# Two-layer encoder trunk: low halves of the last score tile padded to 128 rows, the boundary's norms issued one or two steps earlier, other PSUM banks for the third output tile

## The chip, the core and the metric

One core of one Trainium2 chip runs the whole kernel. The metric is the device time of one execution in microseconds, from the profiler's clock; lower is better. Three runs of the kernel before took 1560.03, 1561.87 and 1566.96 us, so the median is 1561.87 us.

## What is computed

Two layers over 528 tokens (16 meta tokens and 512 of input) of width 1024, in float32. Each layer norms the tokens, projects them to ten pieces, runs a gated short convolution and a chunkwise retention side by side, merges them by sigmoid gates, projects back with `w_o`, norms that and adds it to the residual. Cut to what matters here:

```python
for l in range(DEPTH):
    xn = _rmsnorm(h, pre_norm_g[l])
    proj = xn @ w_in[l] + b_in[l]
    ...
    y_b = _retention_branch(r_q, r_k, r_v, r_z, ret_gn_g[l], w_ret_out[l])
    y = jax.nn.sigmoid(g_a) * y_a + jax.nn.sigmoid(g_b) * y_b
    y = y @ w_o[l]
    h = h + _rmsnorm(y, post_norm_g[l])
return h[:, N_META:]
```

In the retention branch the queries and keys of a head give scores, the scores are weighted by a decay table, and the weighted scores multiply the values. Four heads per layer, 512 value columns per head.

## The kernel before

**Precision.** Every float32 operand of a large product is split into a high half (a rounded copy, written by ScalarE) and a low half (the rest, written by VectorE), by `split` (L140 to L143). A product is then three passes on TensorE: high by high, high by low, low by high. In the names of the profile `whi` and `wlo` are the halves of a weight, `Xh` and `Xl` those of the layer's input, `Shi` and `Slo` those of a head's scores.

**Work of a layer.** TensorE goes through a fixed list of jobs: `Group` (two input projections by a seven-product block scheme, L279), `RetOut` and `ConvOut` (L244), and at the layer's end the product with `w_o` (L678). Small steps that belong to a job, such as norms, scores (`scores`, L425), value transposes (`vtrans`, L450) and the product of scores and values (`attend`, L484), are put into a queue with a delay: `later(d, fn)` lets `fn` be issued d ticks later, and a tick falls every twelve matmuls or so (`mul`, `mm_tile`, `Std.run`, `wo_half`, `opening` call `tick`). The framework then orders the instructions of each engine by priority and by when it thinks their operands are there, and gives out the buffers. Each engine runs its own list in order.

**Scores by values.** A head's keys lie in five tiles, `JT`; the last, j = 4, has 64 real keys. For it the value tile holds the keys twice: in rows 0 to 63 and again in rows 64 to 127, with the high values above the low ones in `V[4][1]`. So two passes are enough: `V[4][1]` by `Shi` over 128 rows, and `V[4][0]` by `Slo` over 64 rows, which is what these lines of `attend` say:

```python
passes = ((0, 0), (0, 1), (1, 0)) if j < len(JT) - 1 else ((1, 0), (0, 1))
...
if j == len(JT) - 1 and x == 0:
    kn = CHUNK
```

`attend` runs four times per head (once for 128 value columns), so 4 x 4 x 2 = 32 times in all, and the 64-row pass is its last matmul each time.

**The boundary between the layers.** `wo_half` multiplies by `w_o` for the first half of the tokens, then for the second (half 0, half 1). `norms` queues for each half a chain with these steps: `tok("y")` sums squares over the channels with small matmuls (`rstd_token`, L370), VectorE scales the sum (L374) and GpSimd takes the power -0.5 (L375); `spread` puts the factor on all partitions with six small matmuls (L384) and ScalarE copies it out (L387); `resid` scales, adds to the residual and squares (L782, L787, L669, L671); then the same statistics and spread for the next layer's norm (`tok("h")`, `spread`), and `scaled` writes the next layer's input halves (L791, then L142 and L143). `opening` starts the first products of layer 1 on half 0, then on half 1, and needs the halves that `scaled` wrote.

**The tail.** The last layer's product with `w_o` (L1167) takes tokens in four tiles of 128. Tiles 0 and 1 fill both buffers of the PSUM pool `pp` (two banks each) in an interleaved loop; tiles 2 and 3 then run one after the other, each half of the columns in a bank of `pp`. `begin` (L1183, L1188) reads a bank out on ScalarE and VectorE. The single banks `pa` and `pc` are used by the input projections and idle in the tail.

Of the kernel before, what the change touches and what calls it, by code (L numbers as in the profile page):

```python
# [11 lines left out]
F32 = mybir.dt.float32  # L12
# [3 lines left out]
ALU = mybir.AluOpType  # L16
# [11 lines left out]
CHUNK = 64  # L28
HALF = T // 2
# [13 lines left out]
JT = [(0, 80, 0), (80, 128, 80), (208, 128, 208), (336, 128, 336), (464, 128, 464)]  # L43
SOFF = [0, 528, 976, 1296, 1488]
# [12 lines left out]
def trunk(ctx: ExitStack, tc: tile.TileContext, xT, w_in, binT, w_co, w_ro, w_o, gpre, gpost,  # L57
          gpost_row, convw, convb, gng, cosT, sinT, decay, out):
    nc = tc.nc
# [13 lines left out]
    def nm(s):  # L73
        cnt[0] += 1
        return f"{s}{cnt[0]}"
# [7 lines left out]
    def pslot():  # L83
        return ps.tile([P, 2, 512], F32, tag="pp", name=nm("pp"))

    def bank(tag):
        return ps1.tile([P, 512], F32, tag=tag, name=nm(tag), bufs=2 if tag == "pb" else 1)
# [39 lines left out]
    def later(delay, fn):  # L127
        now[1] += 1
        heappush(queue, (now[0] + delay, now[1], fn))
# [11 lines left out]
    def split(dst_hi, dst_lo, src):  # L141
        nc.scalar.copy(dst_hi, src)  # L142
        nc.vector.tensor_tensor(dst_lo, src, dst_hi.bitcast(F32), op=ALU.subtract)  # L143
# [140 lines left out]
    class Group:  # L284
# [19 lines left out]
        def halves(self, j):  # L304
            if j != 1:
                r = self.raw[j]
                nc.vector.tensor_tensor(r[:, 512:], r[:, 512:], r[:, 0:512], op=ALU.add)  # L307
            self.w[j] = wtile("whi"), wtile("wlo")
            split(*self.w[j], self.raw[j])
# [68 lines left out]
    def spread(dst, y, t0, sc, nch):  # L378

        pp = pslot()  # L380
        per = min(nch, 264 // sc)
        nb = nch // per
        for c in range(nch):
            nc.tensor.matmul(pp[:, c // per, (c % per) * sc:(c % per + 1) * sc], y[:, c:c + 1].to_broadcast([sc, P]),  # L384
                             ident[0:sc, 0:sc], start=True, stop=True)
        with tc.high_priority():
            nc.scalar.copy(dst[:, t0:t0 + nch * sc].rearrange("p (a b) -> p a b", a=nb), pp[:, 0:nb, 0:per * sc])  # L387
# [27 lines left out]
    def scores(l, q, k, k8, Shi, Slo, js):  # L415

        pp = pslot()
        todo = []
        for n, j in enumerate(js):
            k0, kn, q0 = JT[j]  # L420
            cols = QCOLS[l] if j == 0 else Cols(q0, T - q0, 1)
            for dt in range(2):
                for a, (x, y) in enumerate(((0, 0), (0, 1), (1, 0))):
                    for i, sl in cols.pieces():
                        nc.tensor.matmul(  # L425
                            pp[0:kn, n + i, 0:cols.n], k[dt][x][:, k0:k0 + kn] if j < 4 else k8[:, dt * 2 + x, :], q[dt][y][:, sl],
                            start=(dt == 0 and a == 0), stop=(dt == 1 and a == 2),
                        )
            todo.append((n, j, cols))
        for n, j, cols in todo:  # L430
            k0, kn, q0 = JT[j]
            o = cols.t0 - q0
            s = fslot()
            sv = s[0:kn, 0:cols.w]
            with tc.high_priority():
                nc.vector.tensor_tensor(
                    sv.rearrange("p (a b) -> p a b", a=cols.np),
                    pp[0:kn, n:n + cols.np, 0:cols.n],
                    Dsb[0:kn, DOFF[j] + o:DOFF[j] + o + cols.w].rearrange("p (a b) -> p a b", a=cols.np),
                    op=ALU.mult)  # L440
            ss = slice(SOFF[j] + o, SOFF[j] + o + cols.w)
            later(1, lambda kn=kn, ss=ss, sv=sv: split(Shi[0:kn, ss], Slo[0:kn, ss], sv))

    def vtrans(vt, v8, V, js):

# [20 lines left out]
    def attend(l, h, Shi, Slo, V, v, t, sums):  # L466


        banks = [(0, 208), (208, 528)] if l < DEPTH - 1 else [(META, T)]
        pp = pslot()  # L470
        todo = []
        for j, (k0, kn, q0) in enumerate(JT):
            passes = ((0, 0), (0, 1), (1, 0)) if j < len(JT) - 1 else ((1, 0), (0, 1))
            for x, y in passes:
                for b, (s0, s1) in enumerate(banks):
                    lo_, hi_ = max(s0, q0), s1
                    if lo_ < hi_:
                        todo.append((j, x, y, b, lo_, hi_))
        for n, (j, x, y, b, lo_, hi_) in enumerate(todo):
            _, kn, q0 = JT[j]  # L480
            if j == len(JT) - 1 and x == 0:
                kn = CHUNK
            S = (Shi, Slo)[y]
            nc.tensor.matmul(  # L484
                pp[:, b, lo_ - banks[b][0]:hi_ - banks[b][0]],
                V[j][x][0:kn, v * P:(v + 1) * P],
                S[0:kn, SOFF[j] + lo_ - q0:SOFF[j] + hi_ - q0],
                start=not any(t[3] == b for t in todo[:n]),
                stop=not any(t[3] == b for t in todo[n + 1:]),
            )  # L490
        sq = sums if v == 0 else fslot()
        g = gn_sb[:, l, h * 4 + v:h * 4 + v + 1]
        with tc.high_priority():
            for b, (s0, s1) in enumerate(banks):
                nc.scalar.activation(sq[:, s0:s1], pp[:, b, 0:s1 - s0], AF.Square)
            for b, (s0, s1) in enumerate(banks):
                nc.vector.scalar_tensor_tensor(t[:, s0:s1], pp[:, b, 0:s1 - s0], g, t[:, s0:s1], op0=ALU.mult, op1=ALU.mult)
            if v:
                qs = slice(banks[0][0], T)
                nc.vector.tensor_tensor(sums[:, qs], sums[:, qs], sq[:, qs], op=ALU.add)  # L500
# [271 lines left out]
    def norms(l, half, hts, ysum, hsum, R2, R):  # L772

        sl = slice(half * HALF, (half + 1) * HALF)
        st = {}

        def tok(key, sums):
            st[key] = rstd_token(sums, half * HALF, 88, 3)

        def scale(k):  # L780
            y = YB[:, k:k + 4, sl]
            nc.vector.tensor_tensor(y, y, R2[:, sl].unsqueeze(1).to_broadcast([P, 4, HALF]), op=ALU.mult)  # L782

        def resid(k):
            if k % 4 == 0:
                scale(k)
            nc.vector.tensor_tensor(hts[k][:, sl], hts[k][:, sl], YB[:, k, sl], op=ALU.add)  # L787
            squares(k, hts[k][:, sl], sl, hsum)

        def scaled(k):  # L790
            nc.vector.scalar_tensor_tensor(YB[:, k, sl], hts[k][:, sl], gpre_sb[:, l + 1, k:k + 1], R[:, sl],  # L791
                                           op0=ALU.mult, op1=ALU.mult)
            split(*plain(half, k), YB[:, k, sl])

        later(2, lambda: tok("y", ysum))
        later(5, lambda: spread(R2, st["y"], half * HALF, 88, 3))
        for k in range(KD):
            later(5, lambda k=k: resid(k))
        later(13, lambda: tok("h", hsum))
        later(16, lambda: spread(R, st["h"], half * HALF, 88, 3))  # L800
        for k in range(KD):
            later(16, lambda k=k: scaled(k))

    def opening(tiles, half, ts):

# [20 lines left out]
    for l in range(DEPTH):  # L826
# [7 lines left out]
        hd = heads(0)  # L834
# [27 lines left out]
        def q_done(ts, hd, h, l, d=8):  # L862
            a, b, hd["q"] = rope(ts, QCOLS[l].t0)
            later(0, a)
            later(2, b)

            def tables():
                hd["S"] = [gr.tile([P, SW], F32R, tag="S", name=nm(x), bufs=2) for x in ("Shi", "Slo")]
                nc.sync.dma_start(Dsb, decay[h])
            later(3, tables)  # L870
            for n, js in enumerate(((0,), (1, 2), (3, 4))):
                later(d + 2 * n, lambda js=js: scores(l, hd["q"], hd["k"], hd["k8"], *hd["S"], js))
# [102 lines left out]
    pa = bank("pa")  # L975
    warm = bank("pc")
    for n in range(9):
        o, a, b = (warm, 0, P) if n < 6 else (pa, (n - 6) * P, min((n - 5) * P, HALF))
# [10 lines left out]
    for ks in (slice(0, 1), slice(1, 2), slice(2, 4), slice(4, 6), slice(6, 8)):  # L989
        nc.sync.dma_start(YB[:, ks, :], xT[ks].rearrange("k p t -> p k t"))  # L990
        j = ks.start // 4
# [4 lines left out]
    for k in range(KD):  # L996
        for half in range(2):
            prescale(0, k, half, YH[:, k, half, :])
        j, kk = k // 4, slice(k % 4 * P, (k % 4 + 1) * P)
# [15 lines left out]
    for n in range(3):  # L1015
        t = fslot()
# [6 lines left out]
    R = fslot()  # L1023
# [11 lines left out]
    hd = jobs[0][0]  # L1035
# [40 lines left out]
    for l in range(DEPTH):  # L1076
# [4 lines left out]
        if l:  # L1081
            hd = jb[0]
# [43 lines left out]
        if not last:  # L1126
# [6 lines left out]
            hsum = gr.tile([P, T + 2], F32, tag="u", name="hsum", bufs=2)[:, 0:T]  # L1133
            R2 = fslot()
            R = fslot()
# [15 lines left out]
        else:  # L1151
# [62 lines left out]
            for t in range(2, SEQ // P):  # L1214
                st = state()
                for half in range(2):
                    o = pslot()[:, 0, :]
                    for k in range(KD):
                        wo_k(o, t, k, half)
                    begin(st, o, half)  # L1220
                if t == 2:
                    finish(sts[0], 0)
                    finish(sts[1], 1)
                finish(st, t)
# [80 lines left out]
```

## Time and profile before

| | |
|---|---|
| runs | 1560.03, 1561.87, 1566.96 us, median 1561.87 us |
| profiled execution | 1560.22 us, its span 1558.4 us |
| TensorE matmul busy | 1537.1 us, 99% of the span |
| VectorE busy | 1166.1 us, 75% |
| ScalarE busy | 912.2 us, 59% |
| GpSimd busy | 18.8 us, 1% |
| DMA | 174.37 MB, 112 GB/s on average |

A matmul's duration in the profile overlaps that of the next one, so the distance between two starts, not the duration, is what a matmul costs. Weight loads have rows of their own (PEld) and normally run beside the matmul before.

### The profile page before, as it was taken

The page shows a single profiled execution, that of the slowest core. Times are in us where ns is not written, and L with a number is a line of the kernel's source. Part 1 is how long each engine was busy: PE and PEld are TensorE (multiplying, and loading weights), DVE is VectorE, ACT ScalarE, POOL GpSimd, SP SyncE. Part 2 cuts the span into 40 slices and gives each one's busy share as a digit, 9 for nine tenths or more (in the row PEclk, how much of TensorE's full clock was granted, in tenths as well). Part 3 has the DMA queues.
Part 4 walks back from the last instruction along what each step waited for, and adds up shares of the span by engine and source line. Part 5 has one row for each costly group of instructions (what it writes and reads, how often), then busy time and mean ns, then how long its engine had stood idle before and what let it go on. Part 6 is the DMA issues. An engine that isn't in the chain of part 4 may idle for free.

```text
span 1558.4 us, 29296 instructions
## 1 busy us (share of the span) xinstructions
PE 1537.1 (99%) x11762; PEld 1487.0 (95%) x11762; DVE 1166.1 (75%) x1702; ACT 912.2 (59%) x1763; POOL 18.8 (1%) x23
## 2 busy tenths in 40 slices
PE   9999999999999999999999999999999999999997
PEld 9999999999999999999999999999999999999986
DVE  6997776886878788857367987769778777996642
ACT  6685665565465467646345766655755655776521
POOL 0000000000000000000000000000000000000000
PEclk9999999999999999999999999999999999999999
DMA  8132332232232333435321223322322323334421
GB/s 270 57 128 75 116 109 96 102 110 91 97 106 89 116 122 125 140 129 181 107 104 62 102 95 109 116 98 99 122 95 89 109 97 120 136 131 141 145 88 54
DMA packets 86039, 174.37 MB, mean 112 GB/s; under 512 B 11280, under 2 KB 15888, under 8 KB 85904
## 3 DMA queue, kind: packets, MB, share of 16 engines
q1 hardware_dynamic: 85760, 172.50, 32.0%
q8 instruction: 92, 1.51, 0.4%
q14 instruction: 43, 0.35, 0.1%
q10 hardware_dynamic: 144, 0.01, 0.0%
HBM read 168.21 MB, written 4.26 MB: 111 GB/s over the span
## 4 chain that ended last, share of the span: by engine, by line
PE 91%; DVE 4%; ACT 2%; DMA 1%; issue 1%; SPq 0%; DVEq 0%; POOLq 0%; ACTq 0%
PE pb L279 29%; PE pp L244 18%; PE pc L279 15%; PE pa L279 7%; PE pp L678 7%; PE pp L484 4%; PE pb L678 3%; PE pp L1167 3%; PE pp L425 2%; DMA raw<-in_w_in 1%; PE pp L450 1%; DVE wlo L143 1%; PE pp L384 1%; PE pp L370 1%; ACT whi L142 1%
## 5 line engine op out<-in xcount | busy, mean ns | idle before, releaser
L143 DVE TENSOR_TENSOR wlo<-raw,whi 128x1024 fp32r<-128x1024 f32 (+2 forms) x358 | 394.0, 1109 | 136.9 <-ACT whi L142 135.3
L142 ACT CAST whi<-raw 128x1024 fp32r<-128x1024 f32 (+2 forms) x358 | 339.7, 959 | 251.1 <-PE pp L244 66.2
L279 PE MATMUL pb<-Xh,whi 128*128 128x264 f32 (+2 forms) x1008 | 289.9, 288 | 3.5 <-ACT pa L335 2.3
L279 PE MATMUL pb<-Xh,wlo 128*128 128x264 f32 (+2 forms) x1008 | 285.7, 283 | 0.0
L279 PE MATMUL pb<-Xl,whi 128*128 128x264 f32 (+2 forms) x1008 | 285.4, 283 | 0.0
L244 PE MATMUL pp<-r,whi 128*128 128x264 f32 (+1 forms) x1152 | 246.1, 321 | 0.0
L279 PE MATMUL pc<-Xh,whi 128*128 128x264 f32 (+2 forms) x672 | 193.8, 288 | 1.8 <-ACT f L325 1.5
L279 PEld LDWEIGHTS pb<-Xh,whi 128*128 128x128 f32 x1008 | 189.8, 188 | 5.7 <-ACT pa L335 3.1
L244 PEld LDWEIGHTS pp<-r,whi 128*128 128x128 f32 x1152 | 177.8, 188 | 15.9 <-ACT whi L142 0.3
L279 PE MATMUL pc<-Xl,whi 128*128 128x264 f32 (+2 forms) x672 | 190.7, 284 | 0.0
L279 PEld LDWEIGHTS pb<-Xl,whi 128*128 128x128 f32 x1008 | 189.8, 188 | 0.6
L279 PE MATMUL pc<-Xh,wlo 128*128 128x264 f32 (+2 forms) x672 | 190.3, 283 | 0.0
L279 PEld LDWEIGHTS pb<-Xh,wlo 128*128 128x128 f32 x1008 | 189.8, 188 | 0.0
L244 PE MATMUL pp<-r,wlo 128*128 128x264 f32 (+1 forms) x576 | 153.2, 321 | 0.0
L307 DVE TENSOR_TENSOR raw<-raw 128x512 f32<-128x512 f32 x168 | 115.3, 688 | 27.8 <-DMA raw<-in_w_in 27.0
L279 PEld LDWEIGHTS pc<-Xh,whi 128*128 128x128 f32 x672 | 126.6, 188 | 3.4 <-ACT f L325 2.8
L279 PEld LDWEIGHTS pc<-Xl,whi 128*128 128x128 f32 x672 | 126.6, 188 | 0.1
L279 PEld LDWEIGHTS pc<-Xh,wlo 128*128 128x128 f32 x672 | 126.5, 188 | 0.0
L244 PEld LDWEIGHTS pp<-r,wlo 128*128 128x128 f32 x576 | 95.5, 188 | 7.9
L314 DVE TENSOR_TENSOR raw<-raw,raw 128x512 f32<-128x512 f32 x84 | 58.0, 690 | 57.6 <-DMA raw<-in_w_in 57.4
L279 PE MATMUL pa<-Xh,whi 128*128 128x264 f32 (+2 forms) x336 | 96.8, 288 | 0.0
L279 PE MATMUL pb<-Xh,whd 128*128 128x264 f32 (+2 forms) x336 | 96.3, 287 | 0.3 <-ACT f L325 0.3
(219 smaller groups left out, 3324.0 us busy)
## 6 DMA issues: line engine op xcount, KB each, us to landing
raw<-in_w_in SPq DMA_DIRECT2D x426, 256.0 KB, 2.9
raw<-in_w_ro SPq DMA_DIRECT2D x32, 512.0 KB, 3.2
raw<-in_w_in SPq DMA_DIRECT2D x20, 512.0 KB, 5.0
raw<-in_w_co SPq DMA_DIRECT2D x16, 512.0 KB, 3.2
raw<-in_w_o SPq DMA_DIRECT2D x16, 512.0 KB, 3.8
Dsb<-in_decay SPq DMA_DIRECT2D x8, 520.0 KB, 4.6
h1d<-f SPq DMA_DIRECT2D x8, 264.0 KB, 4.2
f<-h1d SPq DMA_DIRECT2D x8, 264.0 KB, 5.1
```

The source lines that it names most:

```text
L142: nc.scalar.copy(dst_hi, src)
L143: nc.vector.tensor_tensor(dst_lo, src, dst_hi.bitcast(F32), op=ALU.subtract)
L244: nc.tensor.matmul(banks[i][:, 0:cols.n], wt(k)[:, msl], xs(k)[:, sl], start=(k == 0 and a == 0), stop=(k == nk - 1 and a == 2),)
L279: nc.tensor.matmul(o[:, 0:n], wt[:, k, :], xs[:, blk, k, HALF - n:], start=(first and k == 0 and a == 0), stop=(k == 3 and a == 2), skip_g ...
L307: nc.vector.tensor_tensor(r[:, 512:], r[:, 512:], r[:, 0:512], op=ALU.add)
L314: nc.vector.tensor_tensor(b[:, 0:512], a[:, 512:], c[:, 0:512], op=ALU.add)
L370: nc.tensor.matmul(pp[0:sc, 0, c:c + 1], sums[:, t0 + c * sc:t0 + (c + 1) * sc], ones_d[:, 0:1], start=True, stop=True)
L384: nc.tensor.matmul(pp[:, c // per, (c % per) * sc:(c % per + 1) * sc], y[:, c:c + 1].to_broadcast([sc, P]), ident[0:sc, 0:sc], start=True, ...
L425: nc.tensor.matmul(pp[0:kn, n + i, 0:cols.n], k[dt][x][:, k0:k0 + kn] if j < 4 else k8[:, dt * 2 + x, :], q[dt][y][:, sl], start=(dt == 0 ...
L484: nc.tensor.matmul(pp[:, b, lo_ - banks[b][0]:hi_ - banks[b][0]], V[j][x][0:kn, v * P:(v + 1) * P], S[0:kn, SOFF[j] + lo_ - q0:SOFF[j] + h ...
L678: nc.tensor.matmul(o, wt(k), xs[:, i0:], start=(k == 0 and a == 0), stop=(k == KD - 1 and a == 2))
L1167: nc.tensor.matmul(o, x[:, xs], wo[k][half][w], start=(k == 0 and a == 0), stop=(k == KD - 1 and a == 2))
```

## The change

1. In `scores`, the low half of the last key tile is written for 64 rows instead of 128, and a GpSimd memset in `tables` fills its rows 64 to 127 with zeros when a head's score tiles are opened. `attend` no longer cuts that pass to 64 rows, so all its matmuls for the last tile take 128 rows.
2. In `norms` the delays become smaller: spread and residual 5 to 4, the statistics of the next norm 13 to 12, their spread and the scaling 16 to 14. This holds for both halves.
3. In the tail, the two halves of tile 2 go to banks `pc` and `pa` instead of two buffers of `pp`.

```diff
-            later(1, lambda kn=kn, ss=ss, sv=sv: split(Shi[0:kn, ss], Slo[0:kn, ss], sv))
+            def halves(kn=kn, ss=ss, sv=sv, n=CHUNK if j == len(JT) - 1 else kn):
+                nc.scalar.copy(Shi[0:kn, ss], sv)
+                nc.vector.tensor_tensor(Slo[0:n, ss], sv[0:n], Shi[0:n, ss].bitcast(F32), op=ALU.subtract)
+            later(1, halves)
...
-            if j == len(JT) - 1 and x == 0:
-                kn = CHUNK
...
-        later(5, lambda: spread(R2, st["y"], half * HALF, 88, 3))
+        later(4, lambda: spread(R2, st["y"], half * HALF, 88, 3))
         for k in range(KD):
-            later(5, lambda k=k: resid(k))
-        later(13, lambda: tok("h", hsum))
-        later(16, lambda: spread(R, st["h"], half * HALF, 88, 3))
+            later(4, lambda k=k: resid(k))
+        later(12, lambda: tok("h", hsum))
+        later(14, lambda: spread(R, st["h"], half * HALF, 88, 3))
         for k in range(KD):
-            later(16, lambda k=k: scaled(k))
+            later(14, lambda k=k: scaled(k))
...
+                nc.gpsimd.memset(hd["S"][1][CHUNK:, SOFF[4]:].bitcast(F32), 0.0)
...
-                    o = pslot()[:, 0, :]
+                    o = bank(("pc", "pa")[half]) if t == 2 else pslot()[:, 0, :]
```

How the order of instructions moves. On TensorE, half 0: the spread of y stands 12 matmuls of L678 earlier than before, the statistics of h 13 and their spread 24. For half 1 the statistics of y stand 21 such matmuls later, their spread 12 earlier, the statistics of h 12 and their spread 24 earlier. Outside the boundary and the tail TensorE's order is the same. The first place is TensorE at the end of the product with `w_o` for half 1, where the statistics of h for half 0 are taken; `pp_9648` and `pp_9652` hold the output columns 4 and 5 before and after the change, `pp_9705` and `pp_9717` the columns 6 and 7, and `hsum` is the sum of squares. Before:

```order
L678 MATMUL pp_9705<-r_8935,Xh 128x264
L678 MATMUL pp_9705<-r_8937,Xh 128x264
L678 MATMUL pp_9705<-r_8935,Xl 128x264
L678 MATMUL pp_9705<-Xh,wos_8902 128x264
L370 MATMUL pp_9718<-ones_d,hsum 88x1 [waits DVE_49,Activation_49]
L678 MATMUL pp_9705<-Xl,wos_8902 128x264
L678 MATMUL pp_9705<-Xh,wos_8903 128x264
```

Now:

```order
L680 MATMUL pp_9652<-Xl,r_9193 128x264
L680 MATMUL pp_9652<-Xh,r_9194 128x264
L370 MATMUL pp_9701<-ones_d,hsum 88x1 [waits DVE_49,Activation_49]
L680 MATMUL pp_9717<-r_8938,Xh 128x264 [waits DVE_49]
L680 MATMUL pp_9717<-r_8940,Xh 128x264
```

The statistics moved ahead of columns 6 and 7, whose first matmul now waits for VectorE.

The second place is ScalarE from there to the first inputs of layer 1: L769 (now L771) and L669 (now L671) empty columns 6 and 7, L387 copies the spread factor of half 0, and the casts `Xh<-YB` write the high halves that `opening` reads. Before:

```order
L142 CAST Xh<-raw_9207 128x512 [waits PE_49]
L142 CAST Xh<-raw_9209 128x512 [waits PE_49]
L769 ACTIVATE YB<-pp_9705,gpost_sb 128x264 [waits PE_49]
L387 COPY f_9262<-pp_9762 128x264 [waits DVE_49,PE_49]
L669 ACTIVATE f_9792<-pp_9705 128x264 [waits DVE_49]
L769 ACTIVATE YB<-pp_9705,gpost_sb 128x264
L669 ACTIVATE f_9796<-pp_9705 128x264 [waits DVE_49]
L142 CAST Xh<-YB 128x264 [waits DVE_49] x8
```

Now:

```order
L387 COPY f_9266<-pp_9742 128x264 [waits DVE_49,PE_49]
L142 CAST Xh<-raw_9187 128x512 [waits PE_49]
L142 CAST Xh<-raw_9197 128x512 [waits PE_49]
L142 CAST Xh<-YB 128x264 [waits DVE_49] x4
L142 CAST Xh<-raw_9211 128x512 [waits PE_49]
L771 ACTIVATE YB<-pp_9717,gpost_sb 128x264 [waits PE_49]
L671 ACTIVATE f_9796<-pp_9717 128x264 [waits Activation_49]
L771 ACTIVATE YB<-pp_9717,gpost_sb 128x264
L671 ACTIVATE f_9800<-pp_9717 128x264
L142 CAST Xh<-YB 128x264 [waits DVE_49] x3
```

The copy and four of the eight casts now stand ahead of the emptying of columns 6 and 7.

The third place is TensorE at the start of token tile 2 in the tail; `pp_18019` and `pp_18027` are token tile 1. Before:

```order
L1167 MATMUL pp_18019<-r_17997,Xh 128x512
L1167 MATMUL pp_18019<-r_17996,Xl 128x512
L1167 MATMUL pp_18192<-Xh,r_17849 128x512 [waits DVE_49]
L1167 MATMUL pp_18192<-Xl,r_17849 128x512
L1167 MATMUL pp_18192<-Xh,r_17851 128x512
```

Now:

```order
L1170 MATMUL pp_18027<-r_18005,Xh 128x512
L1170 MATMUL pp_18027<-r_18004,Xl 128x512
L1170 MATMUL pc_18200<-Xh,r_17857 128x512
L1170 MATMUL pc_18200<-Xl,r_17857 128x512
L1170 MATMUL pc_18200<-Xh,r_17859 128x512
```

The order of the matmuls is the same; the wait for VectorE is gone.

On GpSimd the eight memsets stand ahead of a norm's power each, except the first.

## Rows read from the trace of the kernel before

**Rows 1.** The page: busy time by engine; the chain that ended last, by engine.
```profile
PE 1537.1 (99%) x11762; PEld 1487.0 (95%) x11762; DVE 1166.1 (75%) x1702; ACT 912.2 (59%) x1763; POOL 18.8 (1%) x23
...
PE 91%; DVE 4%; ACT 2%; DMA 1%; issue 1%; SPq 0%; DVEq 0%; POOLq 0%; ACTq 0%
```

**Rows 2.** Waits of TensorE for a norm's sums: total us, times, longest us.
```profile
PE pp L370 <- DVE f L500: 1.7, 2, 1.5
```

**Rows 3.** Groups by line and shape: the last key tile's two passes (busy us, mean ns).
```profile
L484 PE MATMUL pp<-Slo,r 64*128 64x64 f32 x32 | 9.4, 294 | 0.0
...
L484 PE MATMUL pp<-Shi,r 128*128 128x64 f32 x32 | 6.9, 216 | 0.0
```

**Rows 4.** Timeline, an attend's end: start us, us, what, matmuls and weight loads.
```profile
119.93 0.33 PE L484 MATMUL pp<-Shi,r 128*128 128x192 f32 x2
120.19 0.29 PE L484 MATMUL pp<-Slo,r 64*128 64x64 f32 x1
120.41 0.39 PE L279 MATMUL pa<-Xh,whi 128*128 128x264 f32 x1
120.64 0.28 PE L279 MATMUL pa<-Xl,whi 128*128 128x264 f32 x1
...
120.19 0.18 PEld L484 LDWEIGHTS pp<-Slo,r 64*128 64x128 f32 x1
```

**Rows 5.** Timeline, scores of the last key tile: weight loads, then the next two matmuls.
```profile
884.32 0.86 PEld L425 LDWEIGHTS pp<-r,r 128*128 128x128 f32 x7
...
885.13 0.37 PE L279 MATMUL pb<-Xh,whd 128*128 128x258 f32 x1
885.33 0.28 PE L279 MATMUL pb<-Xl,whd 128*128 128x258 f32 x1
```

**Rows 6.** Chain of waits at the first head's norm: start us, us, what.
```profile
132.45 3.15 DMA raw<-in_w_in
...
137.98 1.07 PE pp L370 x12
```

**Rows 7.** Timeline of TensorE at the boundary; in brackets the wait before.
```profile
786.08 0.63 PE L370 MATMUL pp<-ones_d,hsum 128*88 128x1 f32 x6
786.57 0.37 PE L678 MATMUL pp<-Xl,wos 128*128 128x264 f32 x1
...
790.89 0.80 PE L384 MATMUL pp<-ident,ny 88*128 88x88 f32 x6
793.40 0.51 PE L678 MATMUL pb<-Xh,whi 128*128 128x264 f32 x2 [1.71 <-ACT Xh L142]
...
821.07 0.39 PE L678 MATMUL pp<-r,whi 128*128 128x264 f32 x1 [1.44 <-ACT r L142]
821.78 0.39 PE L678 MATMUL pp<-r,whi 128*128 128x264 f32 x1 [0.32 <-DVE r L143]
```

**Rows 8.** Chain of waits in the same stretch: 36 matmuls without a wait.
```profile
774.32 4.44 PE pb L678 x36
```

**Rows 9.** Timeline of VectorE and ScalarE at the boundary.
```profile
786.82 0.16 DVE L374 TENSOR_SCALAR nv<-pp 88x3 f32<-88x3 f32 x1 [0.33 <-PE pp L370]
...
809.47 0.83 ACT L820 ACTIVATE f<-pb,bin 128x264 f32<-128x264 f32 x2
```

**Rows 10.** TensorE in the tail: 48 matmuls of the chain, then timeline around the wait.
```profile
1501.85 11.09 PE pp L1167 x48
...
1527.84 0.39 PE L1167 MATMUL pp<-r,Xl 128*128 128x512 f32 x1
...
1529.93 0.50 PE L1167 MATMUL pp<-Xh,r 128*128 128x512 f32 x1 [1.70 <-DVE z L1188]
```

**Rows 11.** GpSimd: a memset, a norm's power; the spread that needs it (chain).
```profile
masks.py:197 POOL MEMSET ident<- 128x128 f32 x1 | 0.2, 205 | 0.3 <-POOLq L1297 0.3
...
140.34 1.71 POOL L375 TENSOR_TENSOR ny<-nv,mhalf 88x6 f32<-88x6 f32 x1 [105.92 <-DVE nv L374]
...
144.99 1.31 PE pp L384 x12
```

## The prediction

> **What bounds the kernel now.** I read the page first: TensorE is busy for 99% of the span and holds 91% of the chain that ended last [rows 1]. So time can come off only where a TensorE start is later than it has to be, or where TensorE waits. I then took the waits of TensorE, of which one at a head's norm matters [rows 2], and the timeline around the three places that the change touches. In the rows the reader should look at starts: in a clean stretch 36 matmuls of 264 columns take 4.44 us, 0.123 us each [rows 8].
>
> **The 64-row pass.** What stands in the trace: after the second of the two `Shi` passes (it starts near 120.04: 119.93 plus 0.33, less the 216 ns of the 64-column form [rows 3, 4]) the 64-row pass starts at 120.19, the next projection matmul at 120.41 and the one after at 120.64 [rows 4]. These are steps of 0.15, 0.22 and 0.23, in all 0.60 us for three matmuls. The reason can be seen in the weight load: the load of 64 rows starts at 120.19 together with its own matmul, and not one matmul ahead. In rows 3 the form takes 294 ns against 216 ns for the 128-row form with as many columns. It occurs 32 times.
>
> After the change all three are 128-row matmuls. The nearest rows for that are the scores of the last key tile, also 64 columns and 128 rows and followed by a projection: seven loads end 0.86 us after the first starts, and one load lasts 0.19, so the load starts are (0.86 - 0.19) / 6 = 0.112 apart. They pace the matmuls, and after them the first long matmul starts 0.20 before the next (885.13 to 885.33) [rows 5]. So the three steps become 0.112 + 0.112 + 0.20 = 0.43, and an attend gains 0.60 - 0.43 = 0.17 us; 32 of them 5.4 us. Bounds: if the last step too falls to the usual 0.12, 0.25 each, 8.1 us; if the row count is not the reason for the steps, nothing. I take 5.4, because rows 5 have the same shape in the same company.
>
> The Trainium skill says on the page TensorEngine Tiling (Array Packing), Key Properties, that a change of the tiling mode drains the engine; the late load of rows 4 agrees with that, and by it the three steps shrink as taken.
>
> Not all of it reaches the end. In the first head TensorE waits at the norm's sums for VectorE, which waits for weights to arrive: a load of 3.15 us ends shortly before 137.98 [rows 6], and that wait is the longest of its kind, 1.5 us of 1.7 in two [rows 2]. That chain does not pass through the attends, so their 4 x 0.17 = 0.7 us only lengthen the wait. The second of these waits takes back the last attend of another head, 0.2. Left: 5.4 - 0.9 = 4.5 us.
>
> **The zeros.** Eight memsets of 64 x 64 go to GpSimd. A memset of 128 x 128 takes 0.205 us there, and before the power of the first head's norm the engine is idle for 105.92 us [rows 11]: nothing on the path. VectorE writes the same 64 columns for fewer rows: nothing.
>
> **The boundary.** TensorE waits after the spread for half 0 for 1.71 us, since scaling and cast come after it, and again for half 1, 1.44 and 0.32 us [rows 7]: 3.47 us. From the start of the spread to the resumption lie 793.40 - 790.89 = 2.51 us. The change puts 24 matmuls between spread and need, 24 x 0.123 = 2.95 us plus the spread's own pieces. That covers the 2.51 with some to spare; two casts that now stand between copy and first input on ScalarE eat most of the spare. So both waits go.
>
> What is late next: three hand-offs. First, the statistics of h for half 0 stand directly ahead of columns 6 and 7, whose first matmul waits until VectorE has read the sums out of the same PSUM buffer. By rows, the six pieces take 786.57 - 786.08 = 0.49, and the read ends at 786.82 + 0.16 = 786.98, 0.90 after their start [rows 7, 9]: 0.4, with the signal 0.5 us. Second, the second group of half 0's opening starts with the `pb` banks 12 matmuls (1.5 us) earlier than before, while two evictions of 0.83 us together stand behind the residual's squares [rows 9]: I put 0.3. Third, for half 1 the second `pp` buffer is needed six matmuls (0.74 us) after the first; its two evictions, priced like those, take 0.83 and a signal: 0.3. Net: 3.47 - 1.1 = 2.4 us; bounds 0 and 3.5. The vector chain from the first spread to the next statistics moves with them: about the same 96 matmuls lie between, so it stays hidden.
>
> **The tail.** Token tile 2 waits for VectorE to free a `pp` buffer: 1529.93 - 1527.84 = 2.09 between two starts, 1.70 of it the wait, where 48 matmuls of 512 columns otherwise take 11.09, 0.23 each [rows 10]. `pc` and `pa` are idle, so 2.09 - 0.23 = 1.9 us go. TensorE runs on to the end of the kernel in the same order, so what follows shifts with it. Bounds 1.7 and 1.9.
>
> **The sum.** 4.5 + 2.4 + 1.9 = 8.8 us. The profiled execution took 1560.22 us, the median of the three runs is 1561.87, 1.65 higher. I count from between them, 1561.0: **1552.2 us**, or 0.56% less. A measurement of this kernel can tell about 0.5%, 7.8 us, from no change; the forecast lies just beyond.
>
> **Rivals.**
> *Row count costs nothing.* Then the late steps of rows 4 come from short matmuls as such, and padding leaves them. For it: rows 5 also show a slow step (0.20) after short matmuls of full height. Against it: there the load keeps its lead and the step before is 0.112, not 0.22. The time would be 1561.0 - 2.4 - 1.9 = 1556.7. The Trainium skill, on the page TensorE: Matmul & The Clock Gate, in LDWEIGHTS (loading the stationary operand), says that a load's time goes by its columns and not by its rows; by that rule alone the padding gains nothing, and the durations of rows 4 (0.18 for 64 rows) agree with it, their starts do not.
>
> *The boundary's waits only change place.* ScalarE and VectorE run in order, and casts for half 0 now stand ahead of the squares of half 1. Each is needed by a small matmul on TensorE's own list, which stops everything behind it. If the three hand-offs take 3.5 us instead of 1.1, the boundary gives nothing: 1561.0 - 4.5 - 1.9 = 1554.6.
>
> *The heads keep all.* If the last step falls to 0.12 as well and the weight stream follows, 8.1 + 2.4 + 1.9 = 12.4: 1548.6.
>
> *Slower: the memset holds back the power.* It stands on GpSimd's list ahead of the power of a norm, and waits until TensorE has read the previous head's scores. The power ends at 142.05 and its spread starts at 144.99, so the spread has 2.9 us to spare [rows 11]. If memset and release took the engine past that in the six heads with another head of the layer behind them, TensorE would wait in each. It decides only when the power is late by 2.9 + 8.8 / 6 = 4.4 us; at 6 us late it costs 6 x 3.1 = 18.6, which makes 1570.8. Against it: 0.205 us for a larger memset and an idle engine.
>
> **How the numbers follow.** Forecast 0.70, with a range of its own from 1550 to 1554.5; row count nothing 0.07; waits change place 0.12; heads keep all 0.08; memset 0.03. The range of 1548 to 1556.5 takes in the second, third and half of the first rival. Faster by over 0.5% means under 1553.2 from 1561.0: 0.50 of the forecast's 0.70, and the heads' 0.08, so 0.58. The rest of the forecast, row count and changed place make 0.39 for the same. Slower 0.03.
>
> **What would show it.** The form 64*128 is gone from the groups by shape and the three steps after the last `Shi` pass measure near 0.43; the first head's wait at L370 is longer than 1.5 us; behind both spreads of the boundary no wait over 0.5 us is left, and a wait of about 0.5 stands behind the statistics of h; the tail's two starts are 0.23 apart. The prediction is wrong if the steps at an attend's end stay near 0.60, if the boundary shows new waits of 3 us, or if the weight stream's waits (VectorE on DMA) grow in heads other than the first.

## The result and the profile after

The changed kernel took 1552.07 us (median; 1550.04 to 1552.89, four runs), beside it the kernel before 1561.74 (1560.03 to 1566.96). The ratio is 0.9931 with a 95% interval of 0.9905 to 0.9956: faster by 0.69%, at least 0.44% by the interval, and 0.1 us from the forecast of 1552.2. The profiled execution took 1550.04 us, its span 1548.3. The sum was right; several of its terms were not, and one effect was missing from it.

The page after, busy time and chain by engine [rows 1]: TensorE still bounds the kernel, and its busy time fell by 5.7 us.

```profile
PE 1531.4 (99%) x11762; PEld 1485.2 (96%) x11762; DVE 1165.3 (75%) x1702; ACT 910.7 (59%) x1763; POOL 19.8 (1%) x31
...
PE 92%; DVE 4%; ACT 2%; issue 1%; DMA 1%; DVEq 0%; POOLq 0%; SPq 0%; ACTq 0%
```

The groups by shape [rows 3]: the form 64*128 is gone, both passes of the last key tile have 128 rows.

```profile
L486 PE MATMUL pp<-Slo,r 128*128 128x64 f32 x32 | 8.9, 277 | 0.0
...
L486 PE MATMUL pp<-Shi,r 128*128 128x64 f32 x32 | 6.9, 215 | 0.0
```

The end of an attend in the timeline [rows 4]:

```profile
120.27 0.33 PE L486 MATMUL pp<-Shi,r 128*128 128x192 f32 x2
120.41 0.19 PEld L486 LDWEIGHTS pp<-Slo,r 128*128 128x128 f32 x1
120.43 0.28 PE L486 MATMUL pp<-Slo,r 128*128 128x64 f32 x1
...
120.55 0.37 PE L279 MATMUL pa<-Xh,whi 128*128 128x264 f32 x1
...
120.75 0.28 PE L279 MATMUL pa<-Xl,whi 128*128 128x264 f32 x1
```

The second `Shi` pass starts at 120.27 + 0.33 - 0.215 = 120.385. The steps after it are 0.05, 0.12 and 0.20, in all 0.37 us instead of 0.60: 0.23 per attend, 7.3 us for 32.

The waits of TensorE [rows 2]: the first head's wait at L370 grew from 1.5 to 2.7 us, and the waits of the boundary and the tail are gone but for 0.3.

```profile
PE pp L370 <- DVE f L502: 3.1, 2, 2.7
...
PE pp L680 <- DVE nv L374: 0.3, 1, 0.3
```

The timeline behind that longest wait holds what I had not thought of:

```profile
138.83 1.07 PE L370 MATMUL pp<-ones_d,f 128*88 128x1 f32 x12 [2.70 <-DVE f L502]
...
140.00 0.42 PE L279 MATMUL pa<-Xl,whi 128*128 128x264 f32 x1
140.22 0.42 PE L279 MATMUL pa<-Xh,wlo 128*128 128x264 f32 x1
...
143.08 0.40 PE L279 MATMUL pc<-Xh,whi 128*128 128x264 f32 x1
143.30 0.29 PE L279 MATMUL pc<-Xl,whi 128*128 128x264 f32 x1
```

From 140.00 to 143.30 the matmuls start 0.22 apart and not 0.123. The table of stretches has the reason in the column PEclk, third from the end of a row: 0.79 as a mean of the stretch. TensorE ran a part of it at the lower of its two levels, 1.2 GHz.

```profile
100.00:138.00 38.00, 36.13 (x294) 35.92 (x293) 32.02 (x50) 24.87 (x52) 0.15 (x1) 1.00 0.27 94
138.00:146.00 8.00, 7.17 (x51) 7.20 (x52) 4.93 (x8) 2.00 (x4) 1.65 (x1) 0.79 0.12 41
```

(143.30 - 140.00) / 0.22 makes 15 such steps; they cost 15 x (0.22 - 0.123) = 1.5 us. In the profiled execution of the kernel before, the clock stood at 1.00 there:

```profile
138.00:146.00 8.00, 8.00 (x71) 8.00 (x72) 5.56 (x8) 3.70 (x6) 1.71 (x1) 1.00 0.28 100
```

The boundary in the timeline [rows 7]: behind the statistics of h TensorE resumes after 0.88 us (before 0.49); behind both spreads no wait is left.

```profile
783.66 0.56 PE L370 MATMUL pp<-ones_d,hsum 128*88 128x1 f32 x6
784.54 0.51 PE L680 MATMUL pp<-r,Xh 128*128 128x264 f32 x2 [0.32 <-DVE nv L374]
...
787.56 0.80 PE L384 MATMUL pp<-ident,ny 88*128 88x88 f32 x6
788.15 0.49 PE L680 MATMUL pp<-r,Xh 128*128 128x264 f32 x2
...
813.59 0.80 PE L384 MATMUL pp<-ident,ny 88*128 88x88 f32 x6
814.18 0.37 PE L680 MATMUL pp<-Xh 128*128 128x264 f32 x1
```

What the boundary gave in all is read from two places that stand alike in both kernels: the statistics of y for half 0 ahead of it, and the first scores of layer 1 behind it. Before:

```profile
768.63 0.56 PE L370 MATMUL pp<-ones_d,ysum 128*88 128x1 f32 x6
...
871.10 1.08 PE L425 MATMUL pp<-r,r 128*80 128x512 f32 x4
```

After:

```profile
767.87 0.56 PE L370 MATMUL pp<-ones_d,ysum 128*88 128x1 f32 x6
...
866.55 1.10 PE L425 MATMUL pp<-r,r 128*80 128x512 f32 x4
```

The lead grows from 0.76 to 4.55 us, so the boundary gave 3.8.

The tail [rows 10]: 0.24 between the two starts that stood 2.09 apart.

```profile
1519.52 0.40 PE L1170 MATMUL pp<-r,Xl 128*128 128x512 f32 x1
1519.76 0.39 PE L1170 MATMUL pc<-Xh,r 128*128 128x512 f32 x1
```

The first theory was: the padding gives 7.3 us of shorter steps, loses some of it to the first head's wait, and this longer wait brings the low clock; boundary 3.8 and tail 1.85 besides.

### The profile page after: what moved, and what is told of

It is laid out like the page before. It is cut to its first block, busy times and chain, and to the rows that moved or that the text cites. A ratio compares the mean times of both kernels' runs of the same rounds, so it can differ in the third digit from the quotient of the medians.

```text
span 1548.3 us, 29329 instructions
## 1 busy us (share of the span) xinstructions
PE 1531.4 (99%) x11762; PEld 1485.2 (96%) x11762; DVE 1165.3 (75%) x1702; ACT 910.7 (59%) x1763; POOL 19.8 (1%) x31
## 4 chain that ended last, share of the span: by engine, by line
PE 92%; DVE 4%; ACT 2%; issue 1%; DMA 1%; DVEq 0%; POOLq 0%; SPq 0%; ACTq 0%
PE pb L279 29%; PE pp L244 18%; PE pc L279 15%; PE pp L680 8%; PE pa L279 7%; PE pp L486 4%; PE pb L680 3%; PE pp L425 2%; PE pp L1170 2%; PE pp L454 1%; DVE wlo L143 1%; PE pp L384 1%; DMA raw<-in_w_in 1%; PE pp L370 1%; ACT whi L142 1%
```

## The experiments

Each run is compared with runs of the kernel before on the same chip; a gain in us is one less the ratio, times the median of those (1564.29, 1564.09 or 1563.69), with the ends of the interval in brackets.

### One part at a time

`e1_pad`: the kernel before with the changes of `scores`, `attend` and `tables` alone.

> The kernel before with the padding alone (zeros, 128 rows in the last pass of attend). Theory: at each attend's end the three steps go from 0.60 to 0.37 us, 32 x 0.23 = 7.3 us; four of these attends, 0.9 us, lie ahead of the first head's norm and only lengthen its wait, from 1.5 to about 2.5 us, and behind that longer wait the granted clock drops near 139 us as in the changed kernel, which costs some 1.5 us more. So 7.3 - 0.9 - 1.5 = 4.9 us less than before, near 1556.8 for a before of 1561.7. Rival one, the row count costs nothing and the changed kernel's gain sits elsewhere: no difference. Rival two, the clock drop is an accident of that run or comes from the other parts: the wait of about 2.5 us is there, the granted clock stays at 1.00 near 139 us, and the gain is 6.4 us.

Measured 1557.61 us, ratio 0.9952 (0.9939 to 0.9966): 7.5 us [5.3, 9.5] less. The expected 4.9 lies outside the interval. The low stretch near 139 us was in its trace, as foreseen; that it comes from the longer wait is what the next two runs refute. If the kernel before pays for such a stretch too, as those runs say, the sum is 7.3 - 0.9 = 6.4 us, which the interval holds.

`e2_boundary`: the kernel before with the smaller delays alone.

```diff
-        later(5, lambda: spread(R2, st["y"], half * HALF, 88, 3))
+        later(4, lambda: spread(R2, st["y"], half * HALF, 88, 3))
...
-        later(13, lambda: tok("h", hsum))
-        later(16, lambda: spread(R, st["h"], half * HALF, 88, 3))
+        later(12, lambda: tok("h", hsum))
+        later(14, lambda: spread(R, st["h"], half * HALF, 88, 3))
...
```

> The kernel before with the smaller delays of norms alone. Theory: both waits behind the spreads go (1.71, 1.44 and 0.32 us), a wait of some 0.5 us stays behind the statistics of h, the second pp buffer and the pb banks cost nothing, so 3.5 to 3.8 us less than before. By the prediction's own term it is 2.4 us, with two more hand-offs of 0.3 us each to be seen as waits at L678 and L279. Rival, the waits only change place: no difference, and new waits of 3 us in sum at the boundary. The first head's norm keeps its wait of 1.5 us and the granted clock stays at 1.00 there.

Measured 1559.69 us, ratio 0.9970 (0.9958 to 0.9981): 4.7 us [3.0, 6.6] less. Both waits are gone, 0.3 us stays behind the statistics, and nothing at the `pp` and `pb` banks. But at the first head's norm, where this kernel waits as the kernel before does, its timeline and its table of stretches show:

```profile
137.59 1.58 PE L370 MATMUL pp<-ones_d,f 128*88 128x1 f32 x12 [1.60 <-DVE f L500]
139.03 0.57 PE L279 MATMUL pa<-Xh,whi 128*128 128x264 f32 x1
139.40 0.42 PE L279 MATMUL pa<-Xl,whi 128*128 128x264 f32 x1
```

```profile
138.00:146.00 8.00, 8.00 (x45) 8.00 (x45) 3.69 (x6) 1.82 (x3) 1.72 (x1) 0.58 0.20 61
```

So the low clock needs no padding: a wait of 1.60 us was followed by a longer low stretch than that of 2.70 (45 matmuls in these 8 us, against 51).

`e3_tail`: the kernel before with `bank(("pc", "pa")[half])` for token tile 2 alone.

> The kernel before with the other banks for the third output tile alone. Theory: the wait of 1.70 us at the start of token tile 2 goes and nothing takes its place, 1.75 to 1.9 us less than before. Rival, the wait only moves to tile 3, whose buffers of pp are then the first to be used again: less than 0.5 us gained, and a wait at tile 3's first matmul. Everything ahead of the tail stays as before.

Measured 1562.24 us, ratio 0.9990 (0.9978 to 1.0001): 1.6 us [-0.2, 3.4] less, which fits, but timing alone can't tell it from nothing. The trace can: the list of waits has none in the tail. The low clock stands at two places in this trace. One is the first head's norm, behind a wait of 1.6 us:

```profile
138.00:146.00 8.00, 7.25 (x51) 7.28 (x52) 4.85 (x7) 2.06 (x4) 1.71 (x1) 0.79 0.14 47
```

The other is the boundary, behind the wait that this kernel still has:

```profile
795.45 0.81 PE L678 MATMUL pb<-Xh,whi 128*128 128x264 f32 x2 [1.71 <-ACT Xh L142]
...
797.44 0.42 PE L678 MATMUL pb<-Xh,wlo 128*128 128x264 f32 x1
797.66 0.42 PE L678 MATMUL pb<-Xl,whi 128*128 128x264 f32 x1
```

This turned the first theory over. The new one: such a wait of TensorE, with the small matmuls of a norm or a spread beside it, is in many executions and not in all followed by a stretch at 1.2 GHz. The kernel before has two such places, the changed kernel one. Of the traces with the wait at the first head's norm, five of six show the low stretch; of those with the boundary's wait, one of four; the tail's wait of 1.70 us, with no small matmuls beside it, has none behind it in four. The runs of the kernel before bear it out by their mean granted clock (1.000 is 2.4 GHz throughout): 37 of them took 1560.06 us at 1.000 (one run), 1561.12 on average at 0.999 (4), 1563.24 at 0.998 (11), 1564.62 at 0.997 (13), 1565.49 at 0.996 (7) and 1567.25 at 0.995 (one). The profile that the prediction was read from, 1560.22 us at 1.000, was one of the rare executions without a low stretch. (A mean of 0.999 needs none: behind TensorE's last work the clock falls to 1.2 GHz in every trace, which costs nothing.)

### The first head's norm later

`e4_norm_later` (on the changed kernel) and `e5_before_norm_later` (on the kernel before) have the same edit:

```diff
-            later(10, lambda: hd["n"][0]())
-            later(14, lambda: hd["n"][1]())
+            e = h == 0 and l == 0
+            later(12 if e else 10, lambda: hd["n"][0]())
+            later(15 if e else 14, lambda: hd["n"][1]())
             for v in range(4):
-                later(14 + v, lambda v=v: hd["n"][2](v))
+                later((15 if e else 14) + v, lambda v=v: hd["n"][2](v))
```

> The changed kernel with the first head's norm of layer 0 later: its statistics 24 matmuls of the projections later on TensorE's list, its spread 12 later. Theory: the statistics then come after their operand is there; the wait of 2.7 us goes or falls under 0.5, the granted clock stays at 1.00 near 139 us, and the 0.9 us of the attends, the 1.5 us of the wait of before and the 1.5 us of the low clock come back: 2.7 to 4 us less than the changed kernel, near 1548.5. Rival one, what is late is the weight stream behind VectorE and not the norm: the wait moves to a projection (L279 or L142's halves) and the time stays that of the changed kernel. Rival two, the clock drop has nothing to do with the wait: the wait goes but the granted clock still drops in that stretch, gain 2.2 to 2.7 us at most. Risk: the norm's end, late by 12 matmuls, makes a later job wait.

Measured 1548.90 us, ratio 0.9898 (0.9885 to 0.9912). The changed kernel has 0.9924 in the next runs, so this is 0.26% or 4 us less. The wait at L370 is down to 0.4 us, the granted clock is 1.00 in every stretch up to the end of the work, and all four runs have a mean of 0.999 or 1.000. One wait took its place in part, that of the spread for GpSimd:

```profile
PE pp L384 <- POOL ny L375: 1.4, 1, 1.4
```

> The kernel before with the first head's norm of layer 0 later (statistics 24 matmuls of the projections later, their spread 12). Theory: the wait of 1.5 us goes, less some 1 us that the spread waits for GpSimd, and with it the low clock behind that wait; the low clock behind the boundary's waits stays possible. 2 to 3.5 us below the median of before, mean granted clock 0.998 to 0.999 instead of 0.997. Rival, the low clock is not tied to the wait: 0.5 us gained at most, and a low stretch in the first 200 us of the trace all the same.

Measured 1560.41 us, ratio 0.9978 (0.9969 to 0.9987): 3.4 us [2.0, 4.8] less. The wait was 1.5 us, so 0.5 to 3.3 us of the gain lie beyond its length; the mean clocks, 0.998 to 1.000 where the kernel before had 0.995 to 1.000, point to the clock. Six of the ten runs have 0.998, against none of the four of e4_norm_later, which lacks the boundary's waits as well.

`a1_after`: the changed kernel again, beside these.

> The changed kernel once more, so that it stands on the same chip as the next three and beside many runs of the kernel before. Theory (formed on the runs up to here): a wait of TensorE of 1.5 us or more is in most executions followed by a stretch at the lower granted clock; the kernel before has such waits at the first head's norm and at the boundary, the changed kernel only at the first head's norm. So the difference of the medians is the work saved (some 10 us in the traces) plus the boundary's low stretches less what the norm's wait keeps: 11 to 13 us below the median of before, mean granted clock 0.998 against 0.997. Rival, the first comparison's 0.9931 already holds all of it: 9 to 10.5 us.

Measured 1551.86 us, ratio 0.9924 (0.9912 to 0.9936): 11.9 us [10.0, 13.8] less, as the new theory has it. The interval overlaps that of the first comparison and takes in a part of the rival's 9 to 10.5, so this run alone doesn't decide.

### Is it idleness?

`e11_fill`: the changed kernel with needless work ahead of the late statistics.

```diff
...
         pp = pslot()
+        for n in range(fill):
+            nc.tensor.matmul(pp[:, 1, 0:HALF], Xh[:, 0, 0, 0:P], Xh[:, 0, n % 4, :], start=True, stop=True)
...
```

> The changed kernel with 21 needless products (Xh by Xh, 264 columns, into the unread half of the norm's own bank pair) ahead of the first norm's statistics. They take 21 x 0.123 = 2.6 us, about the wait of 2.5 to 2.7 us, and their operands are there long before: the norm comes no earlier, but TensorE is busy instead of idle. Theory, the idle time brings the low clock: no low stretch near 139 us, mean granted clock 0.999 to 1.000 in all runs, 1 to 2 us less than the changed kernel (1551.9). Rival, the low clock comes at that place whatever TensorE does before it: the low stretch stays in most runs, and the time is that of the changed kernel or up to 0.5 us more.

Measured 1549.34 us, ratio 0.9910 (0.9894 to 0.9925), some 2 us under the changed kernel's 0.9924; the two intervals overlap, so the trace and the clock decide. Its timeline and table of stretches:

```profile
135.90 2.69 PE L370 MATMUL pp<-Xh 128*128 128x264 f32 x21
138.43 1.04 PE L372 MATMUL pp<-ones_d,f 128*88 128x1 f32 x12
139.33 0.37 PE L279 MATMUL pa<-Xh,whi 128*128 128x264 f32 x1
```

```profile
138.00:146.00 8.00, 8.00 (x73) 8.00 (x72) 5.63 (x8) 3.71 (x6) 1.33 (x1) 1.00 0.30 97
```

The norm comes as late as ever, yet all four runs have 0.999 or 1.000, against 0.997 to 0.999 in the nine of the changed kernel, two of which have 0.999. The profiled execution was the slowest of the four, 1552.40 us, with no low stretch up to the end of the work: the clock is not all that differs between executions. At this place the idle time is the cause of the low clock. The same was not tried at the boundary.

### How many rows

`e8_64rows` and `e6_96rows` are e4_norm_later with the last pass cut in `attend`, zeros and memset kept (here 96):

```diff
+            if j == len(JT) - 1 and x == 0:
+                kn = 96
```

> The kernel with the later first norm (e4_norm_later), zeros and memset kept, but the last pass of each attend reads 64 rows again, as in the kernel before. No wait of 1.5 us lies behind the attends here, so nothing takes their gain back and no low clock disturbs it. Theory: 32 x 0.23 = 7.3 us more than e4_norm_later, steps of 0.60 us. By the prediction's own term 32 x 0.17 = 5.4 us. Rival, most of the gain is taken back by the weight stream: under 4 us.

Measured 1553.83 us, ratio 0.9939 (0.9926 to 0.9953).

> The kernel with the later first norm (e4_norm_later), but the last pass of each attend reads 96 of the 128 rows. Theory one, what costs is a pass of no more than 64 rows: steps and time as with 128 rows, 0.37 us for the three steps. Theory two, any pass with fewer rows than its neighbours costs: steps of 0.60 us as in the kernel before, 7.3 us more than e4_norm_later. It is an open choice; I give theory two 0.35.

Measured 1548.26 us, ratio 0.9899 (0.9884 to 0.9914): the time of 128 rows, and 0.40% or 6.3 us less than with 64 rows. That is 1 us under the expected 7.3, which the two intervals allow; besides, e6_96rows has the spread's wait for GpSimd (1.5 us in its trace), which e8_64rows lacks. The groups by shape, first of 96 rows:

```profile
L488 PE MATMUL pp<-Slo,r 96*128 96x64 f32 x32 | 8.9, 277 | 0.0
```

Of 64 rows:

```profile
L488 PE MATMUL pp<-Slo,r 64*128 64x64 f32 x32 | 9.4, 294 | 0.0
```

In the timelines the load of 96 rows starts ahead of its matmul, that of 64 rows together with it:

```profile
118.79 0.19 PEld L488 LDWEIGHTS pp<-Slo,r 96*128 96x128 f32 x1
118.82 0.28 PE L488 MATMUL pp<-Slo,r 96*128 96x64 f32 x1
```

```profile
119.34 0.18 PEld L488 LDWEIGHTS pp<-Slo,r 64*128 64x128 f32 x1
119.34 0.29 PE L488 MATMUL pp<-Slo,r 64*128 64x64 f32 x1
119.56 0.19 PEld L279 LDWEIGHTS pa<-Xh,whi 128*128 128x128 f32 x1
119.56 0.39 PE L279 MATMUL pa<-Xh,whi 128*128 128x264 f32 x1
```

The load behind the 64-row pass, of 128 rows, is late in the same way, so the pass costs on entering and on leaving. In the trace of e8_64rows all 64 loads of these two kinds start 0.003 us or less ahead of their matmul; in that of e6_96rows the loads at the 96-row pass start 0.026 us or more ahead, and those at the 80-row passes, which have more columns, 0.09 or more. So it is not fewer rows as such that cost, but the pass of 64 among passes of 128. The Trainium skill, on the page TensorEngine Tiling (Array Packing), Available Configurations, lists arrangements of the array with 128, 64 and 32 rows; by Key Properties there a change of the mode drains the engine. The runs agree, if a pass of 96 rows counts as one of 128.

### A version that beats both

`e9_norm_16` is e4_norm_later with the spread and the finish at 16 instead of 15; `e10_best` has `later(13, lambda: tok("h", hsum))` besides.

> The kernel with the later first norm (e4_norm_later), whose spread is moved another 12 matmuls later. Theory: the wait of 1.4 us that the spread there still has for GpSimd goes, nothing takes its place: 1 to 1.4 us less than e4_norm_later, near 1547.5, mean granted clock 0.999 to 1.000. Rival, the wait only moves to the products that need the normed head (L244) or to an eviction: no difference.

> e9_norm_16 with the statistics of h at the boundary one tick later again (13, as in the kernel before; the other smaller delays kept). Theory: the wait of 0.3 us behind the statistics goes, since twelve matmuls of columns 6 and 7 then stand between; 0.3 us less than e9_norm_16, which timing can't tell apart. Rival, the spread (14) then comes too close behind the statistics and waits 1 us for the power: slower than e9_norm_16 by 0.5 to 1 us.

Measured 1547.01 us, ratio 0.9889 (0.9872 to 0.9905), and 1546.75 us, 0.9889 (0.9874 to 0.9903). The spread's wait is gone in both, the wait behind the statistics in the second, and nothing took their places; the two can't be told apart. Against the changed kernel's 0.9924 it is another 0.35%, some 5 us.

## Why the prediction was right, and where its steps were off

**The attends.** The mechanism was right: the 64-row pass made three steps late, and 128 rows cure it. "So the three steps become 0.112 + 0.112 + 0.20 = 0.43" is the term that was mis-sized: they became 0.37, and an attend gave 0.23 instead of 0.17. I took the first step from the scores, where a row of short matmuls is paced by its loads. In an attend the two matmuls of 64 columns follow longer ones, and the load of the second is under way early enough (120.41, its matmul 120.43): the first step is 0.05. So 7.3 us instead of 5.4. The rivals here fall: "row count costs nothing" with e8_64rows, and "the heads keep all" with its 8.1 us, since the first head's wait took its part back.

**The loss in the heads.** "Only lengthen the wait" held, 0.9 predicted. The first head's wait grew by 1.2 us, 4 x 0.23 = 0.9 of it from the attends, and the second's by 0.2. What the step did not see is what such a wait costs beside its length.

**The zeros.** Nothing, as said: the memset ahead of the first head's power, which clears the second head's rows, takes 0.15 us and starts almost 10 us ahead of that power.

```profile
131.66 0.15 POOL L871 MEMSET Slo<- 64x64 f32 x1 [96.63 <-PE pp L486]
141.25 1.65 POOL L375 TENSOR_TENSOR ny<-nv,mhalf 88x6 f32<-88x6 f32 x1 [9.45 <-DVE nv L374]
```

**The boundary.** Both waits went, and the first hand-off came with 0.88 - 0.49 = 0.4 us for the 0.5 put down. The second and third (0.3 each) show no wait at all. And a wait removed gave more than its own length: from the first spread's start to the next long matmul it took 2.51 us before [rows 7] and takes 788.15 - 787.56 = 0.59 now, 1.92 less for a wait of 1.71. So 3.8 instead of 2.4. The rival of changed places falls with e2_boundary.

**The tail.** 1.9 predicted, 2.09 - 0.24 = 1.85 in the trace.

**The sum.** At full clock the change saves about 7.3 - 1.1 + 3.8 + 1.85 = 11.9 us, not 8.8, and it also removes the boundary's low stretches. Against that stand the low stretch that stays at the first head's norm, and a base that knew nothing of the clock: 1561.0 lay near the median of the few runs shown, but 37 later ones of the kernel before have a median of 1564.20. Gains too small by 3 us and a base too low by as much nearly cancelled. So the direction and the size of the gain follow from the steps, but that 1552.2 lies so near 1552.07 is luck.

## What to carry to other kernels

Look at the granted clock of several executions, not of one: a wait of TensorE that looks like 1.5 us in a clean profile may cost about twice that in other runs, so taking it away, or filling it with useful work, is worth more than its length. A short pass of 64 rows among full ones costs 0.23 us, which zeros or even 96 rows save. A gain ahead of a wait that something else ends is lost; move the waiting step first.

## What the runs showed of the hardware

**The clock behind a wait.** Waits of 1.60, 1.71 and 2.70 us, each with small matmuls beside it, were followed by stretches at 1.2 GHz in the traces of e2_boundary, e3_tail and the changed kernel; in the profiled execution of the kernel before, waits of 1.5 and 1.71 were not. The same place can go either way, and that makes most of the spread from 1560 to 1567 us: over the 37 runs a straight line on the mean clock takes up 79% of the variance of the time.

**GpSimd behind VectorE.** The power of a norm over 88 x 6 took 1.32 to 2.80 us for the same work. In e4_norm_later it starts while VectorE is in an operation with two inputs:

```profile
142.67 1.21 DVE L143 TENSOR_TENSOR wlo<-raw,whi 128x1024 fp32r<-128x1024 f32 x1
142.90 2.80 POOL L375 TENSOR_TENSOR ny<-nv,mhalf 88x6 f32<-88x6 f32 x1 [11.16 <-DVE nv L374]
...
143.81 0.70 DVE L356 TENSOR_TENSOR f<-f,f 128x528 f32<-128x528 f32 x1
```

VectorE is done at 144.51 and the power 1.19 later. In e8_64rows VectorE is free when the power starts:

```profile
141.21 1.33 POOL L375 TENSOR_TENSOR ny<-nv,mhalf 88x6 f32<-88x6 f32 x1 [10.13 <-DVE nv L374]
141.98 1.23 DVE L143 TENSOR_TENSOR wlo<-raw,whi 128x1024 fp32r<-128x1024 f32 x1 [0.91 <-ACT whi L142]
```

The Trainium skill, on the page SBUF — State Buffer, SBUF: two separate sides, states that the two engines share a pair of ports under an exclusive lock, with VectorE's two-input operations among those that take it. The first trace fits that: the power ends 1.19 us after both operations are done. So it is with the powers over 88 x 6 in all thirteen traces: they take 1.32 to 1.33 us where no such operation runs at their start, and otherwise end 1.19 to 1.21 us after the last of VectorE's operations that follow on each other. The other way round the second trace shows no lock: VectorE's operation starts 0.77 us into the power and takes 1.23 us, against 1.21 in the first. The long power is the wait of 1.4 us that e4_norm_later had left.
